# The last 512 output columns of a retrieved-expert layer: gathered expert rows on VectorE in place of matmuls

## The chip, the cores and the metric

The kernel runs on one core of one Trainium2 chip. The metric is the device time of one execution in microseconds. Before the change it is 2299.76 us, the median of three runs (2298.82 to 2300.3 us).

## The reference, cut to what matters

The kernel computes one decoder layer for 256 tokens of width 2048: token-mixing branches first, then a channel mixer of 16,384 experts (PEER), each one neuron. The change is in the second part:

```python
def peer(xn, w_peer_q, peer_keys, peer_u, peer_v):
    ...
    s_top, i_top = lax.top_k(scores, 16)                       # two halves of a key, 128 keys each
    cand = s_top[..., 0, :, None] + s_top[..., 1, None, :]     # 8 heads, 256 sums for each
    top_s, pos = lax.top_k(cand, 16)                           # 16 experts a head: 128 slots a token
    idx = ...                                                  # i0 * 128 + i1
    gates = softmax(top_s)
    act = gelu(einsum('td,thkd->thk', xb, peer_u[idx]))
    return einsum('thk,thkd->td', gates * act, peer_v[idx])    # 2048 output columns
```

So each token needs 128 of the 16,384 rows of `peer_u` and 128 of `peer_v`. Everything is float32.

## The kernel before, in words

The kernel doesn't gather. It computes all experts for all tokens and lets a zero gate remove those not chosen. The experts stand in 128 groups of 128 (i0 is the group, i1 the partition). Every float32 product is made of three matmuls on rounded halves: a value is split into `hi` (ScalarE copies it with rounding, L84) and `lo` (VectorE subtracts, L85), and hi·hi, hi·lo and lo·hi are summed in PSUM.

All weights come through one stream, `run`: SyncE loads a unit of 128 x 1024 values (`raw`, four buffers), `parts_of` splits it into two chunks of 512 columns (`hi`, `lo`, four buffers each), and a consume function issues the matmuls one unit behind. The split of a chunk therefore waits until TensorE has left the chunk four places earlier. Work in the list `side` is handed out between units at a rate that `run` is given. The instructions of each engine are then put into one fixed order by the scheduler, which can move them far from where the code stands; at run time each engine works through its own list in that order.

The experts come in two stages. In the input stage (`u`, 256 units) each group's 128 dot products with all tokens are made (48 matmuls of 256 columns), scaled (L757, tile `zu`) and put through GELU by `act_u`. Beside it VectorE picks the experts of each token, and `scatter` writes the gates into the grid of groups (`wA`, `wB`) by one-hot matmuls, four tokens at a time, multiplying them with the GELU values. In the output stage (`v`, 256 units, from 1594 to 2290 us) the weights of a group are split (`ph`, `pl`) and multiplied with the group's 128 rows of `peer_v`: per unit two chunks, two token halves, three matmuls of 512 columns (L878 to L880). Eight PSUM banks hold the 256 x 2048 sum. At the end eight additions (L891) put the residual on it and eight stores write it.

GpSimd does almost nothing in either stage, and nothing in the output stage.

Of the kernel before, what the change touches and what calls it, by code (L numbers as in the profile page):

```python
# [30 lines left out]
HU = 1024  # L31
QU = 512


@with_exitstack
def hybrid_block_kernel(ctx: ExitStack, tc: tile.TileContext, a, out):
# [304 lines left out]

    # ---- mLSTM q and k: convolution and SiLU
    zqk = mix.tile([P, KT, T + 3], F32, name="zqk")
# [49 lines left out]

    # ---- attention q, k, v token-major, and mLSTM v and o
    aqk = mix.tile([P, NT, 1280], F32, name="aqk", tag="aqk")
# [38 lines left out]

    # ---- sliding-window attention
    NQ = AH + AKV
# [90 lines left out]

    # ---- mLSTM, all pairs of tokens at once under the running maximum
    mlg = mix.tile([P, MH * MD], F32, name="mlg")
# [65 lines left out]

    # ---- gates, branch projections, merge
    gA = mg.tile([P, KT, T], F32, name="gA", tag="gA")
# [46 lines left out]

    # ---- output projection, residual, second norm's sums
    x2h = xx.tile([P, KT, T], F32R, name="xh")
# [40 lines left out]

    # ---------------------------------------------------------------- experts
    X2 = (x2h, x2l)
    exc = pool(ctx, "exc", 1)  # L690
    NS = PH * TOPK
    iot = exc.tile([P, P], F32, name="iot")
    G.iota(iot, pattern=[[1, P]], base=0, channel_multiplier=0, allow_small_or_imprecise_dtypes=True)
    gT = exc.tile([P, T], F32, name="gT")
# [30 lines left out]
    def evac_q(n):  # L725
        def f(ps):
            q = eb.tile([P, T], F32, name="zu")
            V.tensor_mul(q, ps, rb)
            later.append(lambda: score(n, q))
        return f  # L730
# [9 lines left out]
    def wv(i):  # L740
        return W[0][:, i] if i < NA else W[1][:, i - NA]
# [3 lines left out]
    def act_u(i, z):  # L745
        k = done["tok"]
        if k < T:
            S.activation(wv(i)[:, k:], z[:, k:], AF.Gelu)
        if k > 0:
            S.activation(z[:, :k], z[:, :k], AF.Gelu)  # L750
            V.tensor_mul(wv(i)[:, :k], wv(i)[:, :k], z[:, :k])
        done["e"] = i + 1

    def evac_u(i):
        def f(ps):
            z = eb.tile([P, T], F32, name="zu")
            V.tensor_mul(z, ps, rb)  # L757
            later.append(lambda: act_u(i, z))
        return f
# [8 lines left out]

    # ---- top 16 of the 256 sums, their experts and gates
    a16 = tk.tile([P, TOPK], F32, name="a16")  # L770
# [35 lines left out]
    def turn(t):  # L806
# [5 lines left out]
        V.tensor_copy(gT[:, t * P:(t + 1) * P], pi[:, 2 * P:3 * P])  # L812

    for t in range(NT):
        side += [lambda t=t, h=h: pick16(t, h) for h in range(PH)]
        side += [lambda t=t: decode(t), lambda t=t: gates(t)]
        side += [lambda t=t, c=c, h=h: lookup(t, c, h) for c in range(2) for h in range(PH)]
        side += [lambda t=t: turn(t)]
    run(u_units(0, E0), 0.75)
# [5 lines left out]
    TG = 4  # L825
    NAB = 8

    def scatter(t0):
        """gates of TG tokens, spread over the expert grid by two one-hot factors."""
        AB = []  # L830
# [27 lines left out]

    # ---- weighted sum of the expert rows
    acc = [[(psd, pmm)[t].tile([P, QU], F32, name=("sd", "mm")[t]) for q in range(4)] for t in range(NT)]  # L860
    pw = {}
    x1 = xx.tile([P, NT, D], F32, name="xh")
    nc.sync.dma_start(x1, x1d.rearrange("(t p) d -> p t d", p=P))

    def v_consume(i, h):
        def f(parts):
            if h == 0:
                ph = eb.tile([P, T], F32R, name="ph", tag="ab", bufs=NAB)
                pl = eb.tile([P, T], F32R, name="pl", tag="ab", bufs=NAB)
                split(ph, pl, wv(i))  # L870
                pw[i] = (ph, pl)
            ph, pl = pw[i]
            for q in range(HU // QU):
                hi, lo = parts[q]
                for t in range(NT):
                    ts = slice(t * P, (t + 1) * P)
                    o = acc[t][h * 2 + q]
                    PE.matmul(o, ph[:, ts], hi, start=(i == 0), stop=False)  # L878
# [3 lines left out]

    units = []
    for i in range(NE):
        for h in range(2):
            units.append((a["v"][i * P:(i + 1) * P, h * HU:(h + 1) * HU], v_consume(i, h)))
    run(units)
    for q in range(4):
        for t in range(NT):
            o = x1[:, t, q * QU:(q + 1) * QU]  # L890
            V.tensor_add(o, acc[t][q], o)  # L891
            nc.sync.dma_start(out[t * P:(t + 1) * P, q * QU:(q + 1) * QU], o)
# [61 lines left out]
```

## Time and profile before

| | |
|---|---|
| Median of three runs | 2299.76 us |
| The profiled execution: span from its first to its last instruction | 2296.5 us |
| TensorE busy | 2265.1 us, 99% |
| VectorE busy | 1640.0 us, 71% |
| ScalarE busy | 1343.3 us, 58% |
| GpSimd busy | 64.2 us, 3% |
| Mean DMA rate | 181 GB/s |
| TensorE's granted clock | 0.999 of full speed |

The profiled execution's span is 3.3 us shorter than the median of the runs. Busy time of TensorE is modelled from overlapping matmuls, each of which is shown longer than the distance to the next; how fast it goes is read from the distance between starts. PE is TensorE, PEld its weight loads, DVE VectorE, ACT ScalarE, POOL GpSimd, SP SyncE.

### The profile page before, as it was taken

What the parts mean: (1) busy time and instruction counts of PE and PEld (TensorE: products, weight loads), DVE (VectorE), ACT (ScalarE), POOL (GpSimd) and SP (SyncE); (2) the same over time, 40 slices, a digit from 0 to 9 for tenths busy, and PEclk for the clock granted to TensorE, in tenths of its full rate; (3) what the DMA queues carried; (4) which work ended last, traced back from release to release, by engine and by line L of the source; (5) the groups of instructions that cost most, each with busy time, mean ns of one, the idle gap of its engine ahead of it and who ended that gap; (6) DMA issues with size and microseconds to landing.
All of it is one profiled execution on the core that took longest, in us unless ns stands there. A gap on an engine that the chain in (4) does not pass through costs nothing.

```text
span 2296.5 us, 41687 instructions
## 1 busy us (share of the span) xinstructions
PE 2265.1 (99%) x15441; PEld 2093.2 (91%) x15441; DVE 1640.0 (71%) x3436; ACT 1343.3 (58%) x2915; POOL 64.2 (3%) x79
## 2 busy tenths in 40 slices
PE   7999999999999999999999999999999999999998
PEld 6987799999999999999999999999888888888887
DVE  8977787677779996755677777786655555555555
ACT  6756566566554445554777777775555555555554
POOL 3000000000010020200000000000000000000000
PEclk9999999999999999999999999999999999999999
DMA  6565545556665545555554555556666666665665
GB/s 213 182 196 168 150 156 165 180 181 189 212 219 181 164 157 190 174 183 181 166 164 157 165 161 162 164 159 209 195 193 194 194 193 193 193 195 192 194 193 172
DMA packets 115339, 416.24 MB, mean 181 GB/s; under 512 B 12992, under 2 KB 13120, under 8 KB 114752
## 3 DMA queue, kind: packets, MB, share of 16 engines
q1 hardware_dynamic: 115136, 413.59, 56.5%
q8 instruction: 120, 1.97, 0.3%
q14 instruction: 83, 0.68, 0.1%
HBM read 409.35 MB, written 4.19 MB: 180 GB/s over the span
## 4 chain that ended last, share of the span: by engine, by line
PE 91%; DVE 6%; ACT 1%; issue 1%; POOL 0%; DMA 0%; DVEq 0%; SPq 0%; POOLq 0%; ACTq 0%
PE mm L162 17%; PE mm L160 17%; PE mm L161 17%; PE mm L880 5%; PE mm L878 5%; PE sd L878 5%; PE sd L880 5%; PE sd L879 5%; PE mm L879 5%; PE sd L841 2%; DVE lo L85 2%; PE mm L185 2%; PE mm L186 2%; PE mm L187 2%; ACT hi L84 1%
## 5 line engine op out<-in xcount | busy, mean ns | idle before, releaser
L85 DVE TENSOR_TENSOR lo<-raw,hi 128x512 fp32r<-128x512 f32 x1524 | 1056.2, 695 | 564.4 <-ACT hi L84 537.4
L84 ACT ACTIVATE hi<-raw 128x512 fp32r<-128x512 f32 x1524 | 954.4, 629 | 766.3 <-PE mm L161 374.4
L160 PE MATMUL mm<-xh,hi 128*128 128x256 f32 x3088 | 883.3, 286 | 9.9 <-ACT hi L84 7.4
L162 PE MATMUL mm<-xh,lo 128*128 128x256 f32 x3088 | 877.8, 284 | 9.3 <-DVE lo L85 8.9
L161 PE MATMUL mm<-xl,hi 128*128 128x256 f32 x3088 | 874.8, 283 | 1.1 <-DVE xl L85 1.1
L162 PEld LDWEIGHTS mm<-xh,lo 128*128 128x128 f32 x3088 | 592.2, 192 | 14.3 <-DVE lo L85 13.9
L160 PEld LDWEIGHTS mm<-xh,hi 128*128 128x128 f32 x3088 | 592.8, 192 | 11.5 <-ACT hi L84 8.1
L161 PEld LDWEIGHTS mm<-xl,hi 128*128 128x128 f32 x3088 | 592.9, 192 | 2.1 <-DVE xl L85 1.8
L879 PE MATMUL sd<-lo,ph 128*128 128x512 f32 x512 | 199.2, 389 | 0.0
L878 PE MATMUL sd<-hi,ph 128*128 128x512 f32 x512 | 199.2, 389 | 0.0
L878 PE MATMUL mm<-hi,ph 128*128 128x512 f32 x512 | 199.2, 389 | 0.0
L879 PE MATMUL mm<-lo,ph 128*128 128x512 f32 x512 | 199.2, 389 | 0.0
L880 PE MATMUL sd<-hi,pl 128*128 128x512 f32 x512 | 199.2, 389 | 0.0
L880 PE MATMUL mm<-hi,pl 128*128 128x512 f32 x512 | 199.2, 389 | 0.0
L880 PEld LDWEIGHTS mm<-hi,pl 128*128 128x128 f32 x512 | 96.1, 188 | 20.0
L878 PEld LDWEIGHTS mm<-hi,ph 128*128 128x128 f32 x512 | 96.1, 188 | 20.0
L879 PEld LDWEIGHTS sd<-lo,ph 128*128 128x128 f32 x512 | 96.1, 188 | 20.0
L880 PEld LDWEIGHTS sd<-hi,pl 128*128 128x128 f32 x512 | 96.1, 188 | 19.9
L879 PEld LDWEIGHTS mm<-lo,ph 128*128 128x128 f32 x512 | 96.1, 188 | 19.9
L878 PEld LDWEIGHTS sd<-hi,ph 128*128 128x128 f32 x512 | 96.1, 188 | 19.9
L835 ACT ACTIVATE ab<-iot,i1T 128x128 f32<-128x128 f32 x256 | 89.7, 387 | 0.5 <-DVE i1T L811 0.5
L185 PE MATMUL mm<-hi,xh 128*128 128x512 f32 x224 | 89.4, 400 | 0.0
(272 smaller groups left out, 2436.3 us busy)
## 6 DMA issues: line engine op xcount, KB each, us to landing
raw<-u SPq DMA_DIRECT2D x256, 512.0 KB, 3.8
raw<-v SPq DMA_DIRECT2D x256, 512.0 KB, 4.6
raw<-w_g SPq DMA_DIRECT2D x64, 512.0 KB, 4.0
raw<-w_tok SPq DMA_DIRECT2D x56, 512.0 KB, 4.2
raw<-w_qk SPq DMA_DIRECT2D x32, 512.0 KB, 3.9
raw<-w_o SPq DMA_DIRECT2D x32, 512.0 KB, 4.5
raw<-w_pq SPq DMA_DIRECT2D x32, 512.0 KB, 3.9
raw<-w_pa SPq DMA_DIRECT2D x16, 512.0 KB, 3.6
```

The source lines that it names most:

```text
L84: S.activation(hi, src, AF.Copy)
L85: V.tensor_sub(lo, src, hi.bitcast(F32))
L160: PE.matmul(ps, hi[:, w], xh[:, k], start=(k == 0), stop=False)
L161: PE.matmul(ps, hi[:, w], xl[:, k], start=False, stop=False)
L162: PE.matmul(ps, lo[:, w], xh[:, k], start=False, stop=(k == kts - 1))
L185: PE.matmul(ps, xh[:, k, ts], hi, start=(k == 0), stop=False)
L186: PE.matmul(ps, xh[:, k, ts], lo, start=False, stop=False)
L187: PE.matmul(ps, xl[:, k, ts], hi, start=False, stop=(k == KT - 1))
L835: S.activation(B, iot, AF.Square, bias=i1T[:, t:t + 1])
L878: PE.matmul(o, ph[:, ts], hi, start=(i == 0), stop=False)
L879: PE.matmul(o, ph[:, ts], lo, start=False, stop=False)
L880: PE.matmul(o, pl[:, ts], hi, start=False, stop=(i == NE - 1))
```

## The change

The matmuls of the output stage keep the first 1536 columns (`VQ` = 3 chunks a group). `peer_v` is laid out anew, so that the stream has 192 units of two chunks. The last 512 columns are kept as a table of rows, `vg`, and for each token half (128 tokens, one a partition) and each of its 128 slots one indirect DMA from GpSimd (`fetch_row`) brings each token its own row, 512 values, into one of twelve slabs. VectorE multiplies the slab with the slot's weight, one value a partition, and adds it to `accg` (`gather`): 256 such steps.

The slot's weight is gate times GELU. To have it by slot, `act_u` stores each group's scaled dot products `z` to memory (`zd`, 128 KB a group, from ScalarE's DMA queue), and `fetch_z` brings one value a token and slot back, one indirect DMA for each slot: 256 of them, one 4-byte value for each partition. Sixteen slots make a step of `weigh`: a GELU on ScalarE, a product on VectorE. `addresses` computes the row numbers and the places in `zd` and stores them (`ixd`, with the gates in `gtd`). Slabs, `accg`, weights and addresses lie in the space of `xh` and `xl`, which the input stage holds until its end. The `ab` buffers that the scatter and the split weights share go from eight to six. Line numbers below are those of the changed kernel.

```diff
+VQ = 3
+DG = VQ * QU
...
+    tok = exc.tile([P, NT], F32, name="tok")
+    G.iota(tok, pattern=[[P, NT]], base=0, channel_multiplier=1, allow_small_or_imprecise_dtypes=True)
+    ixd = dram.tile([P, NT, 2 * NS], U32, name="ixd")
+    gtd = dram.tile([P, NT, NS], F32, name="gtd")
+    zd = dram.tile([NE * P * T, 1], F32, name="zd")
...
         if k > 0:
-            S.activation(z[:, :k], z[:, :k], AF.Gelu)
-            V.tensor_mul(wv(i)[:, :k], wv(i)[:, :k], z[:, :k])
+            gz = eb.tile([P, T], F32, name="gz", tag="zu", bufs=4)
+            S.activation(gz[:, :k], z[:, :k], AF.Gelu)
+            V.tensor_mul(wv(i)[:, :k], wv(i)[:, :k], gz[:, :k])
+        S.dma_start(zd[i * P * T:(i + 1) * P * T, 0:1].rearrange("(p t) o -> p (t o)", t=T), z)
...
-            z = eb.tile([P, T], F32, name="zu")
+            z = eb.tile([P, T], F32, name="zu", bufs=4)
...
+    def addresses(t):
+        ix = tk.tile([P, 2 * NS], U32, name="ix")
+        V.scalar_tensor_tensor(iv[:, 0], iv[:, 0], float(NK), iv[:, 1], op0=OP.mult, op1=OP.add)
+        V.tensor_copy(ix[:, 0:NS], iv[:, 0])
+        V.tensor_scalar(ix[:, NS:], iv[:, 0], float(T), tok[:, t:t + 1], op0=OP.mult, op1=OP.add)
+        S.dma_start(ixd[:, t], ix)
+        S.dma_start(gtd[:, t], iv[:, 2])
...
-    NAB = 8
+    NAB = 6
...
-    acc = [[(psd, pmm)[t].tile([P, QU], F32, name=("sd", "mm")[t]) for q in range(4)] for t in range(NT)]
+    acc = [[(psd, pmm)[t].tile([P, QU], F32, name=("sd", "mm")[t]) for q in range(VQ)] for t in range(NT)]
+    vx = xx.tile([P, KT, T], F32, name="xh")
+    got = xx.tile([P, KT, T], F32, name="xl")
+    slab = [got[:, 2 * j:2 * j + 2].rearrange("p a b -> p (a b)") for j in range(8)]
+    slab += [vx[:, 2 * j:2 * j + 2].rearrange("p a b -> p (a b)") for j in range(4)]
+    accg = vx[:, 8:12].rearrange("p (t a) b -> p t (a b)", t=NT)
...
+    nc.sync.dma_start(ixs, ixd)
+    nc.sync.dma_start(wsl, gtd)
+    slots = [(t, s) for t in range(NT) for s in range(NS)]
+    AHEAD = len(slab)
...
+    def fetch_row(k):
+        t, s = slots[k]
+        G.indirect_dma_start(out=buf(k), out_offset=None, in_=a["vg"],
+                             in_offset=bass.IndirectOffsetOnAxis(ap=row_ix[:, t, s:s + 1], axis=0))
+
+    def fetch_z(t, h):
+        for s in range(h * TOPK, (h + 1) * TOPK):
+            G.indirect_dma_start(out=zsl[:, t, s:s + 1], out_offset=None, in_=zd[:],
+                                 in_offset=bass.IndirectOffsetOnAxis(ap=z_ix[:, t, s:s + 1], axis=0))
+
+    def weigh(t, h):
+        hs = slice(h * TOPK, (h + 1) * TOPK)
+        S.activation(zsl[:, t, hs], zsl[:, t, hs], AF.Gelu)
+        V.tensor_mul(wsl[:, t, hs], wsl[:, t, hs], zsl[:, t, hs])
+
+    def gather(k):
+        t, s = slots[k]
+        if s % TOPK == 0:
+            weigh(t, s // TOPK)
+            nh = k // TOPK + 2
+            if nh < NT * PH:
+                fetch_z(nh // PH, nh % PH)
+        w = wsl[:, t, s:s + 1]
+        if s == 0:
+            V.tensor_scalar(accg[:, t], buf(k), w, None, op0=OP.mult)
+        else:
+            V.scalar_tensor_tensor(accg[:, t], buf(k), w, accg[:, t], op0=OP.mult, op1=OP.add)
+        if k + AHEAD < len(slots):
+            fetch_row(k + AHEAD)
+
+    for k in range(AHEAD):
+        fetch_row(k)
+    fetch_z(0, 0)
+    fetch_z(0, 1)
+    side += [lambda k=k: gather(k) for k in range(len(slots))]
...
+    def v_consume(u):
         def f(parts):
...
+            for j in range(2):
+                i, q = divmod(2 * u + j, VQ)
...
+                if q == 1 and i + 1 < NE:
+                    split_w(i + 1)
...
                 for t in range(NT):
                     ts = slice(t * P, (t + 1) * P)
-                    o = acc[t][h * 2 + q]
+                    o = acc[t][q]
                     PE.matmul(o, ph[:, ts], hi, start=(i == 0), stop=False)
                     PE.matmul(o, ph[:, ts], lo, start=False, stop=False)
                     PE.matmul(o, pl[:, ts], hi, start=False, stop=(i == NE - 1))
...
-    run(units)
-    for q in range(4):
+    NU = NE * VQ // 2
+    vu = [(a["v"][u], v_consume(u)) for u in range(NU)]
+    run(vu[:10], 0)
+    run(vu[10:], len(slots) / (NU - 14))
...
+    drain()
+    for q in range(D // QU):
         for t in range(NT):
             o = x1[:, t, q * QU:(q + 1) * QU]
-            V.tensor_add(o, acc[t][q], o)
+            V.tensor_add(o, acc[t][q] if q < VQ else accg[:, t], o)
```

What the scheduler makes of it shows in each engine's order. First VectorE, a little behind the start of the output stage, where the first gather stands. Before (`pl` and `lo` are split halves of weights and of `peer_v`, the numbers are buffers):

```order
L85 TENSOR_TENSOR pl_21660<-wA_8737,ph_21659 128x256
L85 TENSOR_TENSOR lo_21512<-raw_21505,hi_21511 128x512
L85 TENSOR_TENSOR lo_21534<-raw_21531,hi_21533 128x512
L85 TENSOR_TENSOR lo_21538<-raw_21531,hi_21537 128x512
L85 TENSOR_TENSOR lo_21556<-raw_21553,hi_21555 128x512
L85 TENSOR_TENSOR pl_21708<-wA_8737,ph_21707 128x256
L85 TENSOR_TENSOR lo_21560<-raw_21553,hi_21559 128x512
```

and now (L910 is the product in `weigh`, L921 and L923 are gathers into `accg`, which is a part of `xh`; the slabs are parts of `xl` and `xh`):

```order
L87 TENSOR_TENSOR lo_21807<-raw_21804,hi_21806 128x512
L87 TENSOR_TENSOR lo_21811<-raw_21804,hi_21810 128x512
L910 TENSOR_TENSOR xh_21520<-xh_21520 128x16
L921 TENSOR_SCALAR xh_21520<-xl_21521,xh_21520 128x512
L923 SCALAR_TENSOR_TENSOR xh_21520<-xl_21521,xh_21520 128x512
L87 TENSOR_TENSOR lo_21849<-raw_21846,hi_21848 128x512
L923 SCALAR_TENSOR_TENSOR xh_21520<-xl_21521,xh_21520 128x512
L87 TENSOR_TENSOR lo_21853<-raw_21846,hi_21852 128x512
L923 SCALAR_TENSOR_TENSOR xh_21520<-xl_21521,xh_21520 128x512
L87 TENSOR_TENSOR lo_21859<-raw_21856,hi_21858 128x512
L923 SCALAR_TENSOR_TENSOR xh_21520<-xl_21521,xh_21520 128x512
```

Before, nothing but splits stood there. Now a gather stands behind nearly every `lo`. In the list the first gather stands behind the 20th `lo` of the stage and the last behind the 280th of 384; the remaining 104 have no gather between them. The code hands out 1.44 gathers a unit, to the end; the list has about two a unit.

Second GpSimd. Before, its list ended with the lookup of the expert numbers (L795) in the input stage:

```order
L673 TENSOR_TENSOR sqa<-sqa,sq 128x256 x14
L771 IOTA a_10075 128x16
L673 TENSOR_TENSOR sqa<-sqa,sq 128x256
L693 IOTA iot 128x128
L795 TENSOR_TENSOR oh<-oh,itf 128x256 x32
L950 UNCONDITIONAL_BRANCH
L950 ISA
```

and now, where the last fetch of `z` stands (L899 is `fetch_row`, L904 `fetch_z`; the waits are shown, DMASW0 to DMASW7 are the eight semaphores that GpSimd's DMAs use in turn):

```order
L899 DMA xl_21521<-vg,xh_21520 128x512 [waits DMASW2_49,DVE_49]
L904 DMA xh_21520<-zd_8737,xh_21520 128x1 [waits DMASW3_49]
L899 DMA xl_21521<-vg,xh_21520 128x512 [waits DMASW4_49,DVE_49]
L904 DMA xh_21520<-zd_8737,xh_21520 128x1 [waits DMASW5_49]
L904 DMA xh_21520<-zd_8737,xh_21520 128x1 [waits DMASW6_49]
L899 DMA xl_21521<-vg,xh_21520 128x512 [waits DMASW7_49,DVE_49]
L904 DMA xh_21520<-zd_8737,xh_21520 128x1 [waits DMASW0_49]
L899 DMA xl_21521<-vg,xh_21520 128x512 [waits DMASW1_49,DVE_49]
L899 DMA xl_21521<-vg,xh_21520 128x512 [waits DMASW2_49,DVE_49]
L899 DMA xl_21521<-vg,xh_21520 128x512 [waits DMASW3_49,DVE_49]
```

There are 256 of each. Each one waits until the one eight places earlier has landed; a row's fetch also waits for VectorE to leave the slab, which is the gather twelve rows earlier. The 256th fetch of `z` stands behind the 209th row: 465 indirect DMAs up to there, and 47 rows behind it.

Third ScalarE, around the last of the sixteen GELUs on slot values. Before, there was nothing but splits here:

```order
L84 ACTIVATE ph_25019<-wA_8737 128x256
L84 ACTIVATE hi_24871<-raw_24865 128x512
L84 ACTIVATE hi_24893<-raw_24891 128x512
L84 ACTIVATE hi_24897<-raw_24891 128x512
L84 ACTIVATE hi_24915<-raw_24913 128x512
L84 ACTIVATE ph_25067<-wA_8737 128x256
L84 ACTIVATE hi_24919<-raw_24913 128x512
```

and now (L909 is the GELU, which waits for all eight DMASW semaphores, that is for its sixteen `z` values):

```order
L86 ACTIVATE ph_24814<-wA_8742 128x256
L86 ACTIVATE hi_24770<-raw_24768 128x512
L86 ACTIVATE hi_24774<-raw_24768 128x512
L909 ACTIVATE xh_21520<-xh_21520 128x16
L86 ACTIVATE hi_24800<-raw_24798 128x512
L86 ACTIVATE ph_24862<-wA_8742 128x256
L86 ACTIVATE hi_24804<-raw_24798 128x512
L86 ACTIVATE hi_24828<-raw_24826 128x512
```

The sixteenth GELU stands behind the 224th `hi` of the stage, so 160 of the 384 splits stand behind it in ScalarE's list.

## Rows read from the trace of the kernel before

**Rows 1.** Page: busy time of the engines over the span

```profile
span 2296.5 us, 41687 instructions
PE 2265.1 (99%) x15441; PEld 2093.2 (91%) x15441; DVE 1640.0 (71%) x3436; ACT 1343.3 (58%) x2915; POOL 64.2 (3%) x79
```

**Rows 2.** Windows of the expert-input stage, 50 us each, and of the output stage

```profile
core 0: us, PE busy (x) PEld busy (x) DVE busy (x) ACT busy (x) POOL busy (x), PEclk, DMA share, GB/s
1150.00:1200.00 50.00, 50.00 (x422) 50.00 (x421) 36.37 (x84) 39.37 (x121) 0.00 (x0) 1.00 0.48 159
1900.00:2050.00 150.00, 150.00 (x664) 124.20 (x663) 88.10 (x138) 78.00 (x138) 0.00 (x0) 1.00 0.61 193
```

**Rows 3.** TensorE's timeline: start of the output stage, its middle, its end

```profile
start us, us, engine line op out<-in xcount [idle before <-releaser]
1594.05 0.40 PE L878 MATMUL sd<-hi,ph 128*128 128x512 f32 x1
...
1700.16 0.39 PE L878 MATMUL sd<-hi,ph 128*128 128x512 f32 x1
1701.52 0.39 PE L878 MATMUL sd<-hi,ph 128*128 128x512 f32 x1
...
2290.17 0.39 PE L880 MATMUL mm<-hi,pl 128*128 128x512 f32 x1
```

**Rows 4.** Groups of VectorE, then ScalarE, in 1610 to 2280 us

```profile
line engine op names shapes xcount | busy us, mean ns | idle before us <-releasers
L85 DVE TENSOR_TENSOR lo<-raw,hi 128x512 fp32r<-128x512 f32 x493 | 341.8, 693 | 248.9 <-ACT hi L84 237.1
L85 DVE TENSOR_TENSOR pl<-wA,ph 128x256 fp32r<-128x256 f32 x74 | 31.5, 425 | 16.7 <-ACT ph L84 16.7
...
L84 ACT ACTIVATE hi<-raw 128x512 fp32r<-128x512 f32 x493 | 309.7, 628 | 259.9 <-DVE lo L85 181.2 <-PE mm L880 78.7
```

**Rows 5.** VectorE's timeline at 65 us and behind the last split

```profile
65.12 0.48 DVE L352 SCALAR_TENSOR_TENSOR ac<-zqk,acol,ac 128x256 f32<-128x256 f32 x1
65.51 0.69 DVE L85 TENSOR_TENSOR lo<-raw,hi 128x512 fp32r<-128x512 f32 x1
66.11 0.48 DVE L352 SCALAR_TENSOR_TENSOR ac<-zqk,acol,ac 128x256 f32<-128x256 f32 x1
...
2290.02 0.68 DVE L891 TENSOR_TENSOR xh<-sd,xh 128x512 f32<-128x512 f32 x1
2290.61 0.68 DVE L891 TENSOR_TENSOR xh<-mm,xh 128x512 f32<-128x512 f32 x1
```

**Rows 6.** SyncE's timeline at the start: DMA instructions back to back

```profile
1.19 0.42 SPq L236 DMA_DIRECT2D xt<-xT  x1
1.66 0.42 SPq L89 DMA_DIRECT2D raw<-w_qk  x1
2.12 0.43 SPq L236 DMA_DIRECT2D xt<-xT  x1
```

**Rows 7.** DMA issues: size, median us from issue to landing

```profile
raw<-v SPq DMA_DIRECT2D x256, 512.0 KB, 4.6
...
gcol<-gcol SPq DMA_DIRECT2D x1, 16.0 KB, 1.7
```

**Rows 8.** Groups of GpSimd, and VectorE's subtraction beside GpSimd's start-up work

```profile
L795 POOL TENSOR_TENSOR oh<-oh,itf 128x256 f32<-128x256 f32 x32 | 30.9, 985 | 233.9 <-DVE oh L793 233.9
L245 POOL TENSOR_TENSOR sq<-xt 128x256 f32<-128x256 f32 x5 | 3.5, 693 | 0.0
...
L85 DVE TENSOR_TENSOR xl<-xg,xh 128x256 fp32r<-128x256 f32 x32 | 24.1, 771 | 0.5 <-ACT xh L84 0.5
```

**Rows 9.** Windows in which many loads were in flight at once

```profile
10.00:15.00 5.00, 2.70 (x11) 2.40 (x12) 5.00 (x13) 3.08 (x8) 3.08 (x5) 1.00 1.03 415
1600.00:1605.00 5.00, 5.00 (x24) 4.14 (x23) 2.44 (x4) 1.69 (x3) 0.00 (x0) 1.00 0.96 388
```

**Rows 10.** Waits in 1100 to 1590 us: total, times, longest

```profile
DVE ab L837 <- PE sd L841: 7.0, 19, 0.4
```

More of the change, by code (lines that the diff above doesn't have):

```diff
@@ L726, in f @@
         def f(ps):
-            q = eb.tile([P, T], F32, name="zu")
+            q = eb.tile([P, T], F32, name="zu", bufs=4)
             V.tensor_mul(q, ps, rb)
@@ L817, in hybrid_block_kernel @@
         side += [lambda t=t, c=c, h=h: lookup(t, c, h) for c in range(2) for h in range(PH)]
-        side += [lambda t=t: turn(t)]
+        side += [lambda t=t: turn(t), lambda t=t: addresses(t)]
     run(u_units(0, E0), 0.75)
@@ L857, in hybrid_block_kernel @@
     drain()
-    acc = [[(psd, pmm)[t].tile([P, QU], F32, name=("sd", "mm")[t]) for q in range(4)] for t in range(NT)]
-    pw = {}
-    x1 = xx.tile([P, NT, D], F32, name="xh")
-    nc.sync.dma_start(x1, x1d.rearrange("(t p) d -> p t d", p=P))
-    def v_consume(i, h):
-        def f(parts):
[L867 to L874, printed above, removed]
+    acc = [[(psd, pmm)[t].tile([P, QU], F32, name=("sd", "mm")[t]) for q in range(VQ)] for t in range(NT)]
@@ new lines, in hybrid_block_kernel @@
+    vx = xx.tile([P, KT, T], F32, name="xh")
[3 more added lines that the diff above has]
+    accg = vx[:, 8:12].rearrange("p (t a) b -> p t (a b)", t=NT)
+    wsl = vx[:, 12:13].rearrange("p a (t s) -> p (a t) s", s=NS)
+    zsl = vx[:, 13:14].rearrange("p a (t s) -> p (a t) s", s=NS)
+    ixs = vx[:, 14:16].bitcast(U32)
@@ new lines, in hybrid_block_kernel, with buf @@
+    row_ix, z_ix = ixs[:, :, 0:NS], ixs[:, :, NS:]
+    nc.sync.dma_start(ixs, ixd)
+    nc.sync.dma_start(wsl, gtd)
+    slots = [(t, s) for t in range(NT) for s in range(NS)]
+    AHEAD = len(slab)
+    def buf(k):
+        return slab[k % AHEAD]
+    def fetch_row(k):
[6 more added lines that the diff above has]
+                                 in_offset=bass.IndirectOffsetOnAxis(ap=z_ix[:, t, s:s + 1], axis=0))
@@ new lines, in hybrid_block_kernel, with split_w @@
+    for k in range(AHEAD):
[3 more added lines that the diff above has]
+    side += [lambda k=k: gather(k) for k in range(len(slots))]
+    pw = {}
+    def split_w(i):
+        ph = eb.tile([P, T], F32R, name="ph", tag="ab", bufs=NAB)
+        pl = eb.tile([P, T], F32R, name="pl", tag="ab", bufs=NAB)
+        split(ph, pl, wv(i))
+        pw[i] = (ph, pl)
+    def v_consume(u):
+        def f(parts):
+            for j in range(2):
+                i, q = divmod(2 * u + j, VQ)
+                if i == 0 and q == 0:
+                    split_w(0)
+                if q == 1 and i + 1 < NE:
+                    split_w(i + 1)
+                ph, pl = pw[i]
+                hi, lo = parts[j]
@@ L881, in v_consume @@
         return f
[L883 to L886, printed above, removed]
-    run(units)
-    for q in range(4):
+    NU = NE * VQ // 2
+    vu = [(a["v"][u], v_consume(u)) for u in range(NU)]
+    run(vu[:10], 0)
+    run(vu[10:], len(slots) / (NU - 14))
+    x1 = wA[:, 0:NT * D // T].rearrange("p i t -> p (i t)").rearrange("p (t d) -> p t d", d=D)
+    nc.sync.dma_start(x1, x1d.rearrange("(t p) d -> p t d", p=P))
+    drain()
+    for q in range(D // QU):
         for t in range(NT):
             o = x1[:, t, q * QU:(q + 1) * QU]
-            V.tensor_add(o, acc[t][q], o)
+            V.tensor_add(o, acc[t][q] if q < VQ else accg[:, t], o)
             nc.sync.dma_start(out[t * P:(t + 1) * P, q * QU:(q + 1) * QU], o)
@@ L942 @@
         "u": z["peer_u"].reshape(NE, P, KT, P).transpose(0, 3, 2, 1).reshape(NE, P, D),
-        "v": z["peer_v"],
+        "v": z["peer_v"][:, :DG].reshape(NE, P, VQ, QU).transpose(0, 2, 1, 3)
+             .reshape(NE * VQ // 2, 2, P, QU).transpose(0, 2, 1, 3).reshape(NE * VQ // 2, P, 2 * QU),
+        "vg": z["peer_v"][:, DG:],
     }
```

## The prediction

> **What bounds the kernel now.** I read the busy shares first, then the windows of each stage, then TensorE's timeline, and last what VectorE and ScalarE wait for. The reader is to see that TensorE is busy 99% of the span at the full granted clock [rows 1, 2], and that in the output stage nothing interrupts it. Its matmuls there start at one even distance: from the first of six (one chunk of 512 columns, two token halves, three products) to the same matmul of the next chunk it is 1701.52 - 1700.16 = 1.36 us [rows 3]. The stage runs from 1594.05 to about 2290.40 us (the last start, 2290.17, and one distance of 0.227 us), that is 696.3 us or 512 chunks of 1.36. VectorE and ScalarE have room: in that stage they are busy 88.1 and 78.0 of 150 us [rows 2], and their idle time ends with each other or with TensorE [rows 4], because the four chunk buffers let them run only so far ahead. So a matmul taken out shortens the stage as long as nothing else becomes slower than 1.36 us a chunk.
>
> **What goes.** 128 of 512 chunks: 128 x 1.36 = 174.1 us of TensorE, so 522.2 us remain. Two of the eight final additions are moved forward: behind the last matmul they start 0.60 us apart [rows 5], so 1.2 us go. With nothing added in the way the run would take 2299.8 - 174.1 - 1.2 = 2124 us.
>
> **What VectorE gets.** Back to back a split of 512 columns takes 0.60 us (65.51 to 66.11) and a multiply-add by a per-partition scalar of 256 columns 0.39 (65.12 to 65.51) [rows 5]. Mean durations are longer than these distances (0.693 for the split [rows 4]), since one instruction's end overlaps the next one's start. For 512 columns I take the split's 0.60 plus the 0.07 by which the scalar form exceeds half a split's cost, 0.67 us. A weight split (0.34 us, its 0.425 [rows 4] less the same overlap of 0.09) comes once in three chunks. Where a gather stands behind each `lo`, a chunk costs VectorE 0.60 + 0.67 + 0.11 = 1.38 us against TensorE's 1.36, so 260 such chunks cost 5 us more than TensorE needs. VectorE is thus full, but scarcely the bound.
>
> **What GpSimd gets.** 512 indirect DMAs, and this decides. No row of before shows one, so call the time that each holds GpSimd c. From below: SyncE issues a load of 128 rows every 0.46 us [rows 6]; that is a DMA instruction without indices, so I take it as the lower end. From above: a load of 128 short rows is in memory 1.7 us after its issue [rows 7]; GpSimd need not wait for landings (eight are allowed in flight), so c should not exceed this. The two lie far apart. The nearest rows of GpSimd itself, one instruction over 128 partitions while VectorE works on two tensors, take 0.985 us, and 0.693 at the start [rows 8]. I take c = 1.07, near the first of these and close to the middle of 0.46 and 1.7.
>
> **How c becomes time.** The code hands gathers out over the whole stage, but the lists in the section on the change do not. The sixteenth GELU stands in ScalarE's list with 160 of the 384 splits behind it, and it waits for the 256th value fetch, which is GpSimd's 465th DMA. So the last 160 chunks cannot begin before GpSimd has issued 465. GpSimd can't begin before the input stage leaves `xh` and `xl` and the addresses have landed: 5 us (a 512 KB load takes 4.6 [rows 7], the addresses are smaller). Behind the 465th come the landing (about 2.5 us, between 1.7 and 4.6 [rows 7]), the GELU, a copy and a subtraction (some 1.5 us), and then 160 x 1.36 = 217.6 us. The output stage is then 5 + 465c + 4 + 217.6 = 227 + 465c, unless TensorE is slower: its 522 us hold up to c = 0.64. Break-even with the old 696.3 us and the 1.2 us of the tail is c = 1.01. At c = 1.07 the stage takes 724.6 us, 28.3 more than before. Earlier waits are inside this: the first GELU needs 28 DMAs, about 38 us into the stage, where VectorE would be there after some 22; GpSimd works on meanwhile.
>
> **What is hidden.** The 128 stores of `z` go out on ScalarE's queue during the input stage, at 0.46 us each [rows 6] 59 us in all; ScalarE is busy 39.4 of 50 us where the stage is fullest, and TensorE has no gap there [rows 2], so this is nothing, or at most those 59 us if each delayed a split. Six `ab` buffers instead of eight: VectorE's waits for the scatter's matmuls come to 7.0 us now, the longest 0.4 [rows 10]; with 64 scatters that is 26 us at worst, and I take nothing. `addresses` adds six small VectorE instructions and four stores once: 1 us. Two of the final stores now stand in SyncE's list among the loads of `v`, each behind an addition that VectorE reaches before it frees the buffer of the next load, so they hold no load up.
>
> **The sum.** Against the profiled execution: 2296.5 + 28.3 - 1.2 + 1 = 2324.6 us of span. The profiled span lies 3.3 us under the median of the runs, so the run comes to 2328 us, 1.2% more than 2299.76.
>
> [...]
>
> **Rivals.** *GpSimd is quick.* If c is under 0.64, TensorE and VectorE set the stage: 522 + 5 us, 2299.8 - 169 - 1.2 + 1 = 2131 us. For it: SyncE's 0.46 us [rows 6], and GpSimd has nothing else to do. Against it: GpSimd's own instructions on 128 partitions take 0.7 to 1 us [rows 8]. Between 0.64 and 1.00 the time grows by 4.65 us for each 0.01, to 2295.
>
> *GpSimd and VectorE get in each other's way.* Beside GpSimd's two-tensor work VectorE's subtraction of 256 columns took 0.771 us in place of the 0.425 of the same shape [rows 4, 8]. In the new stage VectorE reads two tensors almost without a pause, and each indirect DMA reads its indices from SBUF. If each has to wait for one VectorE instruction, c is 1.07 + 0.60 = 1.67, the stage 227 + 777 = 1004 us, and the run 2607 us. It decides from c = 1.3 on (2435 us). Against it: reading 128 indices is little beside a tensor of 256 columns. [...]
>
> *The DMA engines fill up.* The stage would move 100.7 MB of `v` and 67.1 MB of rows. At the 388 to 415 GB/s of the fullest windows [rows 9] that is 404 to 432 us, less than 522. The 32,768 single values come on top: at nothing no bound arises; at the time of a whole 4 KB packet (16 engines at 388 GB/s: 0.169 us) they take 346 us more, the stage 778 and the run 2381 us. Single values must cost less than that, so this decides only for a small c.
>
> *No difference*: c within 0.01 of 1.01.
>
> **Chances.** What this kernel's measurement can tell from no change is about 0.2%. Forecast, c from 1.02 to 1.3: 0.36. Contention, above 1.3: 0.15. DMA engines: 0.03. No difference: 0.05. c from 0.64 to 1.00: 0.26. Quick GpSimd: 0.15. That is 0.41 faster, 0.05 same, 0.54 slower. The range leaves out a tenth on each side: c = 0.68 gives 543 us of stage and 2147 of run, c = 1.4 gives 878 and 2481; so 2150 to 2480. The forecast's own range, on its side of break-even, is 2303 to 2435.
>
> **What would show it.** GpSimd's list: the distance between its DMAs without a wait is c. The wait of `hi` or of the sixteen GELUs (L909) for DMAs should be the longest, TensorE idle in steps of a group of 16 slots up to some 505 us into the output stage and gapless for the 218 us behind it, and the granted clock at its full level still. The forecast is wrong if TensorE's matmuls keep their 1.36 us a chunk through the whole stage (c below 0.64), if VectorE's durations double (contention), or if ScalarE's GELUs wait while GpSimd itself waits for landings (DMA engines).

## The result, and the profile after

The changed kernel takes 2529.16 us (median of four, 2526.96 to 2533.45), the kernel before 2299.39 beside it: ratio 1.1001, interval 1.0986 to 1.1017. It is 10% slower. I had forecast 2328, with a range of 2150 to 2480; the time lies above the range. Of e6 and e15 below, one execution each took far longer than the others (7600.17 and 2622.9 us), and the ratios leave these two out.

The page's first line, against [rows 1]: TensorE is idle an eighth of the span.

```profile
PE 2209.7 (88%) x14673; PEld 1990.0 (79%) x14673; DVE 1702.3 (67%) x3586; ACT 1260.5 (50%) x2803; POOL 589.8 (23%) x592
```

Windows of the output stage (busy us by engine, then granted clock, DMA share, GB/s), against [rows 2]:

```profile
1603.00:1700.00 97.00, 41.65 (x149) 30.88 (x147) 24.26 (x41) 16.20 (x32) 69.23 (x69) 0.69 0.37 123
1700.00:2300.00 600.00, 373.42 (x1211) 262.27 (x1212) 288.12 (x486) 147.94 (x286) 417.66 (x407) 0.76 0.56 179
2300.00:2500.00 200.00, 196.84 (x839) 157.16 (x838) 143.38 (x238) 102.14 (x187) 38.58 (x36) 1.00 0.71 236
```

From 1603 to 2300 us TensorE works 415 of 697 us, with waits between, at a granted clock of 0.69 and 0.76 on average in the first two windows. Only GpSimd is steadily at work: 69.23 + 417.66 us busy, and 0.30 us more ahead of each of 476 DMAs make 630. Behind 2300 TensorE is full again. All but some 15 of the 200 us by which the span exceeds the forecast are lost before.

GpSimd's groups in the stage (count, busy, mean ns, idle before and its releasers), and two pieces of its timeline, without and beside VectorE's work:

```profile
L904 POOL DMA_INDIRECT xh<-zd,xh x256 | 258.4, 1009 | 78.0 <-issue 75.0 <-DMA xh<-zd,xh 2.7 <-DMA xl<-vg,xh 0.3
L899 POOL DMA_INDIRECT xl<-vg,xh x172 | 180.3, 1048 | 750.9 <-PE mm L956 646.4 <-DVE xh L923 48.7 <-issue 45.1
L899 POOL DMA_INDIRECT xh<-vg,xh x84 | 86.8, 1033 | 47.7 <-issue 24.7 <-DVE xh L923 18.9 <-DVE lo L87 3.0
```

```profile
1624.60 0.95 POOL L904 DMA_INDIRECT xh<-zd,xh  x1 [0.30 <-issue]
1625.85 0.94 POOL L904 DMA_INDIRECT xh<-zd,xh  x1 [0.30 <-issue]
...
1716.13 1.30 POOL L904 DMA_INDIRECT xh<-zd,xh  x1 [0.30 <-issue]
1717.73 0.96 POOL L904 DMA_INDIRECT xh<-zd,xh  x1 [0.30 <-issue]
```

A DMA holds GpSimd 0.95 us, and 0.30 us pass to the next: a distance of 1.25 undisturbed (the first two rows) and 1.60 beside VectorE (the third); the longest single DMA is 1.98 us. The mean is (258.4 + 180.3 + 86.8) / 512 + 0.30 = 1.33 us. Single values and rows of 2 KB cost nearly the same, 1.01 and 1.04 us on average. Besides, GpSimd waits 48.7 + 18.9 us for slabs that VectorE has not read.

VectorE itself is no slower than in [rows 4, 5]:

```profile
L87 DVE TENSOR_TENSOR lo<-raw,hi 128x512 fp32r<-128x512 f32 x378 | 260.3, 689 | 288.6 <-issue 134.9 <-ACT hi L86 132.4 <-ACT ph L86 16.5
L923 DVE SCALAR_TENSOR_TENSOR xh<-xl,xh 128x512 f32<-128x512 f32 x171 | 127.5, 746 | 0.1
```

What ScalarE waits for in the stage (total, times, longest), where [rows 4] had VectorE (181.2 us) and TensorE (78.7 us) alone, and a piece of the timeline:

```profile
ACT hi L86 <- remote: 183.2, 37, 14.2
ACT hi L86 <- PE mm L956: 176.2, 157, 4.6
ACT xh L909 <- DMA xh<-zd,xh: 99.5, 9, 20.6
ACT ph L86 <- remote: 63.6, 11, 12.7
```

```profile
1682.29 0.42 ACT L86 ACTIVATE ph<-wA 128x256 fp32r<-128x256 f32 x1 [12.70 <-remote]
...
1689.07 0.63 PE L956 MATMUL mm<-hi,pl 128*128 128x512 f32 x1
1699.11 0.63 ACT L86 ACTIVATE hi<-raw 128x512 fp32r<-128x512 f32 x1 [12.70 <-remote]
```

Nine of the 16 GELUs wait for values as forecast, 99.5 us together. But 183.2 + 63.6 us of splits are released by something the profile doesn't see ("remote"). `ph<-wA` reads no transfer: it needs its buffer back from TensorE. At 1682.29 and 1699.11 TensorE's last matmul is, by its (modelled) end, over for 9.4 us (its ends are 1672.87 and 1689.70). So TensorE's signal that matmuls are done seems to come late by some 9 us. Nothing like it stands in [rows 4]; the experiments had to deal with it.

The sixteenth GELU stands at 2286.49; the span ends 238.7 us later. It does not wait for its values: GpSimd's 465th DMA, the last value fetch, starts at 2278.96, and ScalarE stands until 2283.78 at a weight split that "remote" releases:

```profile
2283.78 0.42 ACT L86 ACTIVATE ph<-wA 128x256 fp32r<-128x256 f32 x1 [9.17 <-remote]
2285.19 1.39 ACT L86 ACTIVATE hi<-raw 128x512 fp32r<-128x512 f32 x2 [0.99 <-remote]
2286.49 0.20 ACT L909 ACTIVATE xh<-xh 128x16 f32<-128x16 f32 x1
```

One more number differs from before. Where nothing waits, near the end of the stage, a chunk takes TensorE 1.40 us (2422.34 - 2420.94) instead of the 1.36 of [rows 3], with GpSimd's last DMA long past:

```profile
2420.94 0.40 PE L954 MATMUL sd<-hi,ph 128*128 128x512 f32 x1
...
2422.34 0.40 PE L954 MATMUL sd<-hi,ph 128*128 128x512 f32 x1
```

### The profile page after: what moved, and what is told of

Read it like the earlier page. It is cut to its first block, busy times and chain, and to the rows that moved or that the text cites. A ratio compares the mean times of both kernels' runs of the same rounds, so it can differ in the third digit from the quotient of the medians.

```text
span 2525.2 us, 41320 instructions
## 1 busy us (share of the span) xinstructions
PE 2209.7 (88%) x14673; PEld 1990.0 (79%) x14673; DVE 1702.3 (67%) x3586; ACT 1260.5 (50%) x2803; POOL 589.8 (23%) x592
## 4 chain that ended last, share of the span: by engine, by line
PE 68%; POOL 9%; issue 9%; DVE 7%; another core or an unknown queue 5%; ACT 1%; DMA 1%; ACTq 0%; DVEq 0%; POOLq 0%; SPq 0%
PE mm L164 16%; PE mm L162 16%; PE mm L163 16%; POOL xh L904 5%; PE sd L859 2%; POOL xl L899 2%; DVE lo L87 2%; PE mm L956 2%; PE sd L955 2%; PE sd L954 2%; PE mm L187 2%; PE mm L188 2%; PE mm L189 2%; PE sd L956 2%
## 5 line engine op out<-in xcount | busy, mean ns | idle before, releaser
L87 DVE TENSOR_TENSOR lo<-raw,hi 128x512 fp32r<-128x512 f32 x1396 | 964.6, 693 | 596.4 <-ACT hi L86 424.9
L86 ACT ACTIVATE hi<-raw 128x512 fp32r<-128x512 f32 x1396 | 870.6, 628 | 893.0 <-PE mm L163 386.9
L899 POOL DMA_INDIRECT xl<-vg,xh x172 | 180.3, 1048 | 750.9 <-PE mm L956 646.4
L904 POOL DMA_INDIRECT xh<-zd,xh x256 | 258.4, 1009 | 78.0 <-issue 75.0
L956 PE MATMUL sd<-hi,pl 128*128 128x512 f32 x384 | 164.2, 427 | 0.0
L954 PE MATMUL mm<-hi,ph 128*128 128x512 f32 x384 | 163.8, 427 | 0.0
L955 PE MATMUL mm<-lo,ph 128*128 128x512 f32 x384 | 163.8, 427 | 0.0
L956 PE MATMUL mm<-hi,pl 128*128 128x512 f32 x384 | 163.5, 426 | 0.0
L923 DVE SCALAR_TENSOR_TENSOR xh<-xl,xh 128x512 f32<-128x512 f32 x171 | 127.5, 746 | 0.1
L899 POOL DMA_INDIRECT xh<-vg,xh x84 | 86.8, 1033 | 47.7 <-issue 24.7
```

The costliest lines, as they stand in the source:

```text
L86: S.activation(hi, src, AF.Copy)
L87: V.tensor_sub(lo, src, hi.bitcast(F32))
L899: G.indirect_dma_start(out=buf(k), out_offset=None, in_=a["vg"], in_offset=bass.IndirectOffsetOnAxis(ap=row_ix[:, t, s:s + 1], axis=0))
L904: G.indirect_dma_start(out=zsl[:, t, s:s + 1], out_offset=None, in_=zd[:], in_offset=bass.IndirectOffsetOnAxis(ap=z_ix[:, t, s:s + 1], axi ...
L923: V.scalar_tensor_tensor(accg[:, t], buf(k), w, accg[:, t], op0=OP.mult, op1=OP.add)
L955: PE.matmul(o, ph[:, ts], lo, start=False, stop=False)
```

## The experiments

Theory 1: GpSimd's series of DMAs at 1.25 to 1.33 us, with 160 chunks behind the last GELU in the lists. Theory 2: waits between GpSimd, the sum and TensorE. Theory 3: contention. Ratios are against the kernel before in the same runs.

**e1, nothing reads what is fetched.**

```
- side += [lambda k=k: gather(k) ...]
+ (all 512 DMAs issued, no GELU, no sum; TensorE computes all 2048 columns)
```

> All 512 indirect DMAs are issued as in the changed kernel, but nothing reads what they bring; TensorE computes all 2048 columns as the kernel before. Theory 1 (an indirect DMA holds GpSimd some 1.25 to 1.33 us whatever it moves, and nothing else is slowed): the 512 are through after 640 to 680 us, TensorE keeps 1.36 us a chunk, the run stays at 2300 us, give or take 10. Theory 2 (the rest of the changed kernel's loss is waits between GpSimd and the sum): same, with a distance of 1.25 to 1.33 us throughout, since there is nothing to wait for. Theory 3 (the transfers or GpSimd disturb VectorE, ScalarE or TensorE): gaps in TensorE's output stage, a run over 2330 us.

2329.76 us, ratio 1.0127 (1.0111 to 1.0144). A window, a wait of ScalarE and GpSimd's last DMA:

```profile
1700.00:1900.00 200.00, 200.00 (x858) 161.03 (x858) 114.09 (x180) 101.45 (x179) 156.55 (x143) 1.00 0.64 189
```

```profile
ACT hi L86 <- PE mm L961: 280.9, 378, 0.8
```

```profile
2316.58 0.95 POOL L899 DMA_INDIRECT xl<-vg,xh  x1 [0.30 <-issue]
```

```profile
2313.02 0.40 PE L961 MATMUL mm<-hi,pl 128*128 128x512 f32 x1
```

The run is 20 us over theory 1. TensorE is not held up: no gap, full clock, no wait over 0.8 us. But 858 matmuls in 200 us are 1.40 us a chunk, as at the end of the changed kernel, and its last matmul starts at 2313.02 instead of 2290.17 [rows 3]. Since the 1.40 also stands there with GpSimd idle, GpSimd is not needed for it; what it comes from stays open. Some 23 of the 30 us are this; the rest is GpSimd, which ends last: 143 DMAs in 200 us are 1.40 us each. Beside a steady stream of splits the price is 1.40, not 1.33; I had missed that. It is exactly one DMA a chunk, so the rhythm of the splits may set it.

**e2, the gathers alone.**

```
- run(vu[:10], 0); run(vu[10:], ...)
+ run(vu[:3], 0)
```

> The output stage keeps the gathers, their GELUs and multiply-adds, but only 6 of its 384 chunks: the other loads, splits and matmuls are left out (1536 output columns lack them). Theory 1: the DMAs still stand 1.25 to 1.33 us apart, the stage takes 9 + 512 x 1.25 to 1.33, 650 to 690 us. Theory 3 (1.33 is the price of company: VectorE's splits, the loads of v): a distance of 1.1 us or less, a stage under 575 us.

2296.32 us. Two DMAs with VectorE idle, and GpSimd's groups:

```profile
1617.45 0.94 POOL L904 DMA_INDIRECT xh<-zd,xh  x1 [0.30 <-issue]
1618.70 0.94 POOL L904 DMA_INDIRECT xh<-zd,xh  x1 [0.30 <-issue]
```

```profile
L904 POOL DMA_INDIRECT xh<-zd,xh x256 | 250.4, 978 | 78.0 <-issue 52.7 <-DMA xh<-zd,xh 25.3
L899 POOL DMA_INDIRECT xl<-vg,xh x172 | 188.0, 1093 | 697.4 <-DMA xh<-ixd 645.3 <-issue 43.3 <-DMA xh<-zd,xh 6.1
L899 POOL DMA_INDIRECT xh<-vg,xh x84 | 90.5, 1078 | 25.6 <-issue 22.6 <-DMA xh<-zd,xh 2.4 <-DVE xh L923 0.3
```

1.25 us without company, so theory 3's 1.1 is out, and the stage is 700 us with hardly any TensorE work: the gather alone is as long as the whole old stage (696.3). The mean is 1.33 here too, with almost no splits or loads: VectorE's multiply-adds are left. The 242 DMAs with no VectorE instruction beside them hold GpSimd 0.94 to 0.95 us, the other 270 on average 1.11. Over all DMAs company adds 0.08 us here and in the changed kernel and 0.15 in e1, and GpSimd pays it: VectorE's split of 512 columns has 0.689 us in the changed kernel and 0.693 before [rows 4]. What in VectorE's work does it no run shows.

**e3, no value fetches.**

```
- if s % TOPK == 0: weigh(...); fetch_z(...)
```

> The value fetches and their 16 GELUs are left out (the gathered columns are weighted by the gates alone), so GpSimd has 256 DMAs instead of 512, with all the bytes of the rows. Theory 1: 256 x 1.33 = 341 us of GpSimd, under TensorE's 522; 119 chunks stand behind the last multiply-add in VectorE's list, 9 + 341 + 162 = 512; so the stage is 525 to 540 us and the run 2130 to 2145. Theory 3 (bytes or VectorE set the pace): the stage stays over 650 us, the run over 2250.

2150.19 us, ratio 0.9347 (0.9332 to 0.9363).

```profile
1700.00:1900.00 200.00, 200.00 (x859) 161.01 (x858) 199.20 (x333) 105.08 (x191) 154.82 (x143) 1.00 1.00 378
```

With half the DMAs and all the bytes of the rows, at 378 GB/s and with VectorE full, TensorE has no gap in this window. The bytes are not the matter. What went is 256 DMAs and, with them, the GELUs that wait for values; e3 does not part the two, but e1 and e2 show what the number alone costs. (5 us over the forecast.)

**e4, gathers pinned.**

```
+ with tc.issue_after(last hi), tc.issue_after(last lo): gather(k)
```

> The same instructions, but each gather is held in the list behind the split that was recorded last, so that only 35 instead of 160 chunks stand behind the sixteenth GELU. Theory 1 (GpSimd's series and the order make the loss): stage 9 + 465 x 1.33 + 4 + 35 x 1.36 = 680, or 9 + 512 x 1.33 + some 15 = 705 where the last rows end it: a run of 2285 to 2320. Theory 2 (waits for slabs and the low granted clock make the loss, and stay when the order changes): over 2400 us.

2392.84 us, ratio 1.0404 (1.0387 to 1.0422): 136 us less than the changed kernel, 73 more than the upper end of theory 1. ScalarE's waits, then VectorE's:

```profile
ACT hi L88 <- PE mm L962: 400.1, 247, 22.6
ACT ph L88 <- PE mm L961: 75.6, 121, 1.9
ACT xh L911 <- DMA xh<-zd,xh: 20.6, 1, 20.6
```

```profile
DVE xh L925 <- DMA xl<-vg,xh: 181.3, 48, 22.3
DVE xh L925 <- DMA xh<-vg,xh: 73.9, 28, 8.3
```

ScalarE has no wait for "remote", and only one GELU waits. Now VectorE waits 255 us for rows: GpSimd's list has stretches of value fetches ahead of the rows that VectorE needs next.

**e5, GpSimd's list fixed too.**

```
+ issue_after(GpSimd's last DMA): one fetch_z, one fetch_row in turn
```

> As the pinned kernel, and GpSimd's own list is fixed as well: one value fetch and one row fetch in turn, 32 values and 12 rows ahead of the sum. Theory 1 (the price of 512 DMAs in a row is the floor, and the waits for slabs of the changed kernel and of the pinned one come from the order of the lists): 9 + 512 x 1.34 + some 20 = 715 us of stage, a run of 2300 to 2325. Theory 2 (the waits for slabs are no matter of order): over 2350 us.

2416.22 us, 1.0509 (1.0492 to 1.0527). Theory 1 fails here. VectorE waits 2.1 us for rows, but this is back:

```profile
ACT hi L88 <- remote: 137.8, 30, 12.7
...
ACT ph L88 <- remote: 27.7, 10, 8.5
```

**e6 and e7, one token half.** 256 DMAs; in e7 rows of 4 KB.

```
- slots = [(t, s) for t in range(NT) for s in range(NS)]
+ slots = [(0, s) for s in range(NS)]     # TensorE: half 1 has all columns
```

> Only the first token half takes its last 512 columns from gathered rows: 256 indirect DMAs instead of 512, and TensorE saves 128 x 0.68 = 87 us of its 696. Order fixed as in the chained kernel. Theory 1: 256 x 1.34 = 343 us of GpSimd lie under 609 us of TensorE; stage 610 to 630, run 2212 to 2230. Theory 3 (company costs VectorE or the loads more): over 2290 us.

> The first token half takes its last 1024 columns from gathered rows of 4 KB: 256 indirect DMAs, and TensorE saves 256 x 0.68 = 174 us. Theory 1 (the price of a DMA on GpSimd does not depend on the bytes): TensorE 522 us, VectorE 512 x 0.60 + 128 x 0.34 + 128 x 1.3 = 517, the loads 201 MB, at the 375 GB/s of the fullest windows of the runs before 537 us; stage 525 to 560, run 2125 to 2165. Rival: the DMA engines or a price by bytes set the pace, over 2200 us.

e6: 2285.35 us, 0.9930 (0.9910 to 0.9949). e7: 2236.77, 0.9734 (0.9714 to 0.9754). They are 0.7% and 2.7% under the kernel before, and 55 and 72 us over their forecasts. A window of e6:

```profile
1633.00:1660.00 27.00, 10.44 (x32) 7.47 (x33) 8.66 (x15) 4.80 (x10) 20.29 (x23) 0.69 0.23 68
```

It loses time here, while GpSimd issues its first 44 DMAs in a row: from 1603 to 1750 us TensorE stands 46 us, and from 1750 on it has no gap. e7 has that too, and ScalarE waits 145.5 us for loads, at 335 to 357 GB/s from 1750 to 2200 us.

**e8, fewer indices.** To see what the price is made of.

```
- out=buf(k), row_ix[:, ...]      z_ix[:, ...]
+ out=buf(k)[0:64], row_ix[0:64, ...]      z_ix[0:16, ...]
```

> As the first run (nothing reads what is fetched, TensorE computes every column), but each row fetch has 64 indices instead of 128 and each value fetch 16. Price by instruction: the DMAs keep 0.95 us undisturbed and a mean distance of 1.39 us. Price by index: row fetches fall to some 0.5 to 0.7 us, value fetches to some 0.15 to 0.4, and GpSimd is through in under 500 us; the run falls from 2330 to 2300 us, since the DMAs no longer end behind TensorE.

2954.26 us, though less is fetched than in e1. Rows of the timeline:

```profile
1648.57 0.85 POOL L904 DMA_INDIRECT xh<-zd,xh  x1 [0.30 <-issue]
...
1702.89 0.63 ACT L86 ACTIVATE hi<-raw 128x512 fp32r<-128x512 f32 x1 [15.47 <-remote]
...
1706.17 0.63 PE L961 MATMUL mm<-hi,pl 128*128 128x512 f32 x1
1719.69 0.63 ACT L86 ACTIVATE hi<-raw 128x512 fp32r<-128x512 f32 x1 [16.17 <-remote]
...
2015.31 1.10 POOL L899 DMA_INDIRECT xh<-vg,xh  x1 [0.30 <-issue]
2016.71 1.10 POOL L899 DMA_INDIRECT xh<-vg,xh  x1 [0.30 <-issue]
...
2201.97 0.91 POOL L899 DMA_INDIRECT xh<-vg,xh  x1 [0.30 <-issue]
```

The price is nearly all by instruction: undisturbed 0.85 us for 16 indices, 0.91 for 64, 0.95 for 128. But VectorE is not the only company: 167 DMAs of this run take more than 1 us (most 1.09 to 1.10, some 1.80) with no VectorE instruction beside them, as the two at 2015 us do. In e2 and in the changed kernel none does, and the cause is not shown. And here the late signals stand alone: no GELU, no sum, and yet a chunk every 16.80 us from 1650 to 2290, as long as GpSimd issues. Then 1.40 us again.

**e9, e10, e13: what the delay goes with.** e9 multiplies one token half, e10 has 128 indices a row again, e13 adds a product.

```
e9:  - for t in range(NT)             + for t in range(1)
e10: - out=buf(k)[0:64], row_ix[0:64  + out=buf(k), row_ix[:
e13: + PE.matmul(o, pl[:, ts], lo, ...)
```

> As the run with fewer rows (nothing reads what is fetched, 64 indices in a row fetch, 16 in a value fetch), but TensorE multiplies only for the first token half: 3 matmuls a chunk instead of 6. In that run TensorE gave back the buffers of one chunk every 16.8 us while GpSimd issued. If TensorE is what is slow there, by matmul, the period falls to 8.4 us and the run to some 2500 us or less; if the delay hangs on something else, once a chunk, it stays at 16.8 us and the run near 2800.

> As the run with fewer rows, but row fetches have all 128 indices again; value fetches keep 16. If the short row fetches set off TensorE's late completions, they are gone here: 1.40 us a chunk throughout and a run of 2300 to 2330 us. If the short value fetches do, TensorE is slow again from the first of them on: over 2700 us. The price of a value fetch with 16 indices should be 0.85 us again, of a row fetch 0.95 undisturbed.

> As the run with fewer rows, which gave back a chunk's buffers every 16.8 us while GpSimd issued, with a fourth product (lo by pl): 8 matmuls a chunk instead of 6 (the result gains a term of rounding size). If the delay goes with the number of TensorE's instructions, the period is 16.8 x 8 / 6 = 22.4 us; if it hangs on something else, once a chunk, 16.8 us stay. The run is about 3100 us in either case (full speed alone would be 512 x 1.81 = 929 us of stage, 2530).

e9: 2284.45 us, faster than both forecasts, no "remote" wait at all; ScalarE waits for loads. e10: 2326.03 us, none either. e13: 3202.40 us, and ScalarE's timeline:

```profile
1904.58 0.63 ACT L86 ACTIVATE hi<-raw 128x512 fp32r<-128x512 f32 x1 [21.77 <-remote]
1926.98 0.63 ACT L86 ACTIVATE hi<-raw 128x512 fp32r<-128x512 f32 x1 [21.77 <-remote]
```

22.40 us for 8 matmuls, 16.80 for 6: 2.80 us a matmul in both. So the delay goes with TensorE's matmuls, not with ScalarE's work or the loads of a chunk, which are the same in both. It can be absent with the same DMAs in another size (e1, e10), and was absent with half the matmuls. What starts it stays open.

**e11, e12: a later start.**

```
e11: - run(vu[:10], 0)   + run(vu[:48], 0)
e12: 768 columns, - run(vu[:10], 0)   + run(vu[:24], 0)
```

> As the kernel with the first token half only and 512 gathered columns, but the sum begins behind 48 loads of v instead of 10, when its first 32 values and 12 rows have long landed. Theory A (the 75 us that it lost in its first 150 us are the wait for the first values): TensorE goes through without a gap, 609 us of stage, a run of 2212 to 2230. Theory B (GpSimd's 44 DMAs in a row are enough to delay TensorE's completions): still 2265 to 2285.

> 768 gathered columns for the first token half, rows of 3 KB, the sum beginning behind 24 loads. TensorE saves 192 x 0.68 = 131 us: 566 us; VectorE 512 x 0.60 + 128 x 0.34 + 128 x 1.0 = 479; 184 MB in 566 us are 325 GB/s, under the 350 to 360 at which the loads of the 1024-column kernel were late. Theory A: a run of 2170 to 2190. Theory B: 2220 to 2250, with the loss in the first 100 us of the stage.

e11: 2251.52 us, 0.9793 (0.9777 to 0.9810). e12: 2209.30, 0.9600 (0.9584 to 0.9616). Both lie between the theories: no "remote" wait in either, but a GELU wait of 20.5 and 15.9 us. The first GELU still stood near the stage's start, because a weight split that is ready early was what it was held behind.

**e14, values first, in the changed kernel.** Only the order of the first 44 DMAs.

> The changed kernel with the first 32 value fetches ahead of the first 12 row fetches, nothing else. Theory (order of lists and 465 DMAs set the time): the first GELU's values land 15 us sooner, the rest is as before: 2515 to 2530 us. If TensorE's late completions are a matter of how the first DMAs fall, they may be absent here: ScalarE's waits without a visible releaser, 183 us, are gone and the run is 2430 to 2460 us.

2528.75 us; "remote" still 139.6 + 79.9. This order at the beginning of the series does not decide it.

**e15 and e18, e16: gathers held behind splits of `v`.**

```
- at = last split of any kind
+ at = last split of v;  + pace[0] = 0.0
```

> As the kernel with 768 gathered columns for the first token half, with each gather held behind the last split of v rather than behind a split of the weights, so that the first GELU stands behind 58 splits instead of near the stage's beginning. TensorE 566 us without a gap: a run of 2172 to 2185. If the 20 us wait and the low clock behind it were not the loss: 2205 as before.

> The evenly ordered 768-column kernel once more, for a profile at the full clock: 2212 to 2222 us. If TensorE's late completions are its loss, ScalarE has waits without a visible releaser of 30 to 60 us near the 44 DMAs at the stage's start; if not, the profile shows another wait.

> The full gather (both token halves, 512 columns) in the same even order, GpSimd's list alternating. If nothing but GpSimd's series is left: 9 + 512 x 1.34 + some 15 = 710 us of stage, a run of 2300 to 2320. If TensorE's late completions come as in the first chained kernel: 2390 to 2420.

e15: 2219.67 us, 0.9643 (0.9621 to 0.9665), slower than e12 and than both forecasts. The profile of e18, the same kernel (2222.45 us), shows where time goes, beside GpSimd's first DMAs and with no GELU near (the first stands at 1691 us):

```profile
1633.00:1660.00 27.00, 8.68 (x19) 4.48 (x17) 2.50 (x4) 2.30 (x4) 17.74 (x19) 0.58 0.14 39
```

Up to 1662 us "remote" makes 20.2 us of ScalarE's waits (15.2 for `hi`, 5.0 for `ph`), less than the 30 to 60 expected. e16: 2443.25 us, over even its slower forecast, "remote" 169.3 + 19.5: the full gather in an even order has the late signals again.

**e17, first DMAs paced.**

```
+ V.memset(zsl[:, t, s:s + 1], 0.0)   # behind a split; fetch_z(k) waits for it
```

> As the evenly ordered kernel with 768 gathered columns for the first token half, but the first 32 value and 8 row fetches each wait for a small VectorE instruction behind a split, so that GpSimd issues them over the first 26 loads (70 us) instead of back to back. If back-to-back DMAs beside a full TensorE set off the late completions, none come here: TensorE 566 us without a gap, a run of 2172 to 2185. If they come with any indirect DMA, 2205 to 2225 as before.

2204.16 us, 0.9584 (0.9568 to 0.9600): the fastest version that computes everything, 4% under the kernel before, but not the 2172 to 2185 of the theory; 8.1 us "remote" remain.

```profile
1700.00:2150.00 450.00, 450.00 (x2080) 369.20 (x2079) 391.88 (x614) 268.87 (x503) 229.63 (x199) 1.00 0.93 329
```

Behind 1700 us GpSimd waits for slabs between its DMAs, and TensorE has no gap.

## Why the prediction was wrong

- **c, the step that failed.** I took 1.07 us, from GpSimd's tensor instructions [rows 8]. Those 0.985 us were near: a DMA holds GpSimd 0.95. What I left out is the 0.30 us between one DMA and the next, which no row of before showed, and the 0.08 us (0.15 in e1) that company costs. The 465 DMAs up to the last value take 1.32 us each, which is 117 us more than forecast, most of the miss. By the forecast's own break-even, c = 1.01, the undisturbed 1.25 already made it slower: 227 + 465 x 1.25 = 808 us.
- **GpSimd never waits: the second step that failed.** I had it work on through every wait. c alone would have given 2328 + 117 = 2445 us, still in the range; the waits took it out. GpSimd waits 67.6 us for slabs over the whole stage, and 62 us between its DMAs, 52 of them these, fall before the 465th: VectorE's multiply-adds stand in a list with splits that wait for GELUs and for TensorE's late signals. The two causes are not separated: the one full gather without late signals, e4, waits 56.5 us for slabs in another order.

```profile
POOL xl L901 <- DVE xh L925: 34.1, 21, 2.8
POOL xh L901 <- DVE xh L925: 22.4, 16, 2.9
```

- **Start, landing and tail.** GpSimd's first DMA is at 1603.0, where the forecast, with its 1 us for `addresses`, had 1600: 3 us. From the end of the last value fetch (2279.9) to the sixteenth GELU pass 6.6 us in place of 2.5, because ScalarE still waits for TensorE: 4 us. Behind that GELU stand 239 us, the forecast had 224: 15 us, of which 160 x 0.04 = 6 are the chunk's 1.40 us instead of 1.36. That the 160 chunks count was right; e4, with 35 behind the GELU, is 136 us faster, though it lacks the late signals too, so the two shares are open.
- **Sum.** 3 + 117 + 62 + 4 + 15 = 201 us, which is what lies between the forecast span of 2324.6 us and the profiled 2525.2.
- **The clock.** "At its full level still" was wrong: with TensorE waiting, the granted clock is 0.69 to 0.76 on average before 2300 us.
- **Rivals.** By its bounds (c above 1.3, 2435 us or more) the contention rival came nearer than the forecast, but not by its mechanism: company costs 0.08 to 0.15 us, not the 0.60 that it priced, on top of a floor that I had set too low, and VectorE's own instructions are no longer (the split 0.689 us, before 0.693). Quick GpSimd is out by e2, and the rows' bytes by e3.
- **Right.** Nine GELUs wait for values, GpSimd's series sets the time, and the stage ends with more than 220 us almost without a gap. That TensorE stops in steps of a group of 16 slots holds in part: the late signals add stops of their own.

## What to carry to other kernels

Price a series of indirect DMAs by their number, not their bytes: one needs 1.25 us of GpSimd here, 1.4 beside a busy VectorE (1.40 in e1, 1.39 in e3), and 512 are as long as the stage that they were to shorten. Gather fewer, longer rows (one token half, 768 columns: 256 DMAs, ratio 0.958), and look in the built lists for what stands behind the first and the last wait. When a wait has no visible releaser, look at an engine whose ends the profile models.

## What the runs showed of the hardware

TensorE's done signals seem to come late, in some runs, while GpSimd issues indirect DMAs beside it. A chunk then takes 2.80 us a matmul in e8 and e13 (16.80 us for 6, 22.40 for 8), though the trace shows the matmuls in quick succession: those of a chunk of e8 all start within 2.6 us, the last four 0.42 to 0.43 us apart, at a mean granted clock of 0.53 (0.23 us apart at the full clock). A chunk has as many weight loads as matmuls, 6 in e8 and 8 in e13, so a price by weight load fits as well as one by matmul. In the same stretch of e8 GpSimd's DMAs often start 1.40 us apart with VectorE idle (2015.31, 2016.71). But e1 and e10 have as many matmuls and DMAs and no delay (2329.76 and 2326.03 us against e8's 2954.26); no run here shows the cause.
